# Weight sums written over the raw weights, two borrowed load buffers, and a written step order with 120 fast pairs

## The chip, the cores and the metric

The kernel runs on one core of a Trainium2 chip. The metric is the device time of one execution, in microseconds (us). PE is TensorE, which multiplies matrices; PEld is its weight load; DVE is VectorE, ACT is ScalarE, POOL is GpSimd; SP is SyncE, whose queue issues nearly all loads here.

## What is computed

One encoder layer over 256 tokens of width 4096, in float32. The input projection has 9792 columns; multi-head latent attention and dilated attention run beside each other; their gated outputs go through an output projection; a gated per-layer embedding follows.

```python
h = rms_norm(x, g_mix)
proj = h @ w_in                      # 4096 x 9792
c_q, c_kv, k_rope, gate_a, q_b, k_b, v_b, gate_b = split(proj)
y_a = rms_norm(mla_attention(...), g_out_mla) * silu(gate_a)
y_b = rms_norm(dilated_mixture_attention(q_b, k_b, v_b), g_out_dil) * silu(gate_b)
x = x + concat(y_a, y_b) @ w_out     # 4096 x 4096
gate = sigmoid(rms_norm(x, g_ple) @ w_ple_gate)   # 4096 x 4096
x = x + (p @ w_ple) * gate
return rms_norm(x, g_final)
```

## The kernel before

Every float32 matrix product is done with split numbers: a value is a high half `hi` (rounded by an ACT copy) and a low half `lo` (the rest, by a DVE subtraction), and `mm` (L263) makes one product of three matmuls, hi x hi, hi x lo and lo x hi. Weights arrive as raw float32 tiles of 128 rows x 1024 columns (512 KB) over SP's queue, into four tiles with the tag `raw` (`RAW = 4`, L1887). A step of the program is one such conversion and the matmuls that use it. `fetch`, `convert_one` and the loop at the end keep loads and conversions some steps ahead of the matmuls; converted halves lie in three tiles `wp` and in further tiles of the stage's ring.

The three large projections are cut into blocks of 1024 output columns (class `Block`): six for q, k and v of the dilated attention (two blocks for each), five for the latent and the gates, three of the output projection (the rest of it runs as `Chunk`s), four of the embedding's gate. A block has 32 rows of tiles, and its output is 2 halves of tokens (256 = 2 x 128) by 2 halves of columns (2 x 512), four products for each row of tiles. That is a plain step (`plain_step`). Two rows of tiles can instead be taken as a 2 x 2 block matrix product in Winograd's form, with seven products where plain steps take eight: a fast pair (`fast_steps`). It needs sums of the four parts of the raw weights, which DVE makes, and sums of the activations, which `add_sums` makes once for a stage and which need room. A pair is four steps: M1; M2 and M3; M5 and M7; M6 and M4. The products M1, M5, M6 and M7 go to banks of their own and are added into the four quarters when the block's last pair is done (`d_mid`, `gate_mid`, `out_mid`, `wide_mid`), the other banks at the block's end (`d_done`, `gate_done`, `out_done`, `wide_done`).

Before, the weight sums T[0] and T[1] went into tiles of their own: T5 and T6 in the q/k/v stage, B1 at the gates, B4 and Al1 in the output projection, Ah2 in the last one. The first step of a pair needs both raw tiles; it releases the first one once the step is converted, the second step releases the second:

```python
sub(T[0][:, 0], r[0][:, 1], r[0][:, 0])
sub(T[0][:, 1], r[0][:, 1], r[1][:, 1])
split(hi[:, 0], lo[:, 0], r[0][:, 0])
```

How many pairs a block has stands in lists (`FAST_QKV`, `FAST_G`, `FAST_O`, `FAST_P`), and `spread` orders pairs and plain steps by fixed costs. All instructions are written out by a planner: `Clock` holds a modelled time for each engine, and tasks (attention heads, block ends, sums) are woven between the steps when the modelled times let them.

In `d_mid` and `d_done` the sums of q, k, v and of the latent are scaled by the row's normaliser while they are added (scalar_tensor_tensor on DVE from the banks). In `gate_rest` the gain of the output norm is multiplied in with the gate, head by head.

## Time and profile before

| | before |
|---|---|
| median of 3 runs | 1899.48 us (1897.54 to 1899.76) |
| profiled execution, span | 1897.4 us |
| PE busy | 1878.5 us (99%), 9133 matmuls and transposes |
| PEld busy | 1579.8 us (83%) |
| DVE busy | 1696.8 us (89%), 2354 instructions |
| ACT busy | 1140.2 us (60%), 1543 instructions |
| DMA | 370.59 MB, mean 195 GB/s |

The span is from the first to the last instruction of the profiled execution. Matmuls are pipelined: the busy time of PE takes the modelled end of each, so that short waits between two of them do not show in it.

### The profile page before, as it was taken

Reading aid. Unit: us, or ns where it says so; the run is one execution under the profiler, and the core shown is the slowest. Engines: PE = TensorE matmul, PEld = TensorE weight load, DVE = VectorE, ACT = ScalarE, POOL = GpSimd, SP = SyncE. Lnnn points to the kernel's source line nnn. Section 1 sums busy time; section 2 is a strip of 40 time slices with the busy share of each in tenths; the row PEclk is TensorE's granted clock in tenths of the full one; section 3 lists DMA queues with packets and bytes.
Section 4 is the critical chain, followed back from the end, with each engine's and each line's share of the span. In section 5 each row is a group of like instructions: output and inputs, shape, how many; then the busy total and the mean of one; then the engine's idle time right before and its main releaser. Section 6 shows DMA issues by size and latency. Waiting matters only on the chain.

```text
span 1897.4 us, 25417 instructions
## 1 busy us (share of the span) xinstructions
PE 1878.5 (99%) x9133; PEld 1579.8 (83%) x9133; DVE 1696.8 (89%) x2354; ACT 1140.2 (60%) x1543; POOL 31.2 (2%) x41
## 2 busy tenths in 40 slices
PE   9999999999999999999999999999999999999997
PEld 7888888888899888888888999888888888888885
DVE  6999999899898989999998777999989989989897
ACT  7655656565588555556556556656655555666654
POOL 0000000000011000000000010100000000000000
PEclk9999999999999999999999999999999999999999
DMA  8666666666735566666667553576666666665665
GB/s 279 189 205 213 214 212 200 198 213 193 218 84 159 166 211 183 196 215 189 208 199 209 137 142 123 167 231 204 216 199 217 187 194 218 194 223 183 221 222 180
DMA packets 160871, 370.59 MB, mean 195 GB/s; under 512 B 29116, under 2 KB 70952, under 8 KB 160744
## 3 DMA queue, kind: packets, MB, share of 16 engines
q1 hardware_dynamic: 159896, 366.58, 62.0%
q0 software_dynamic: 512, 1.84, 0.3%
q8 instruction: 72, 1.18, 0.3%
q10 hardware_dynamic: 336, 0.54, 0.1%
q14 instruction: 55, 0.45, 0.1%
HBM read 364.72 MB, written 4.19 MB: 194 GB/s over the span
## 4 chain that ended last, share of the span: by engine, by line
PE 85%; DVE 10%; DMA 2%; issue 2%; ACT 1%; POOL 0%; DVEq 0%; ACTq 0%; POOLq 0%
PE m L177 49%; PE t L177 16%; PE s L177 11%; PE o L177 9%; DVE lo L177 3%; DVE B L177 3%; DVE T L177 2%; DVE Ah L177 1%; DMA raw<-in_w_ple_gate_dram 1%; DVE Al L177 1%; DMA raw<-in_w_in_dram 1%; ACT hi L177 0%; DVE st L177 0%; ACT B L177 0%; DVE B7b L177 0%
## 5 line engine op out<-in xcount | busy, mean ns | idle before, releaser
L177 ACT ACTIVATE hi<-raw 128x1024 fp32r<-128x1024 f32 (+2 forms) x396 | 378.9, 966 | 278.1 <-PE m L177 70.9
L177 DVE TENSOR_TENSOR lo<-raw,hi 128x1024 fp32r<-128x1024 f32 (+2 forms) x396 | 433.4, 1107 | 61.8 <-ACT hi L177 60.6
L177 PE MATMUL m<-hi,Ah 128*128 128x512 f32 (+2 forms) x659 | 247.2, 387 | 0.3 <-ACT hi L177 0.3
L177 DVE TENSOR_TENSOR B<-raw,B 128x1024 fp32r<-128x1024 f32 (+3 forms) x228 | 213.9, 947 | 20.5 <-ACT B L177 18.8
L177 PE MATMUL m<-hi,Al 128*128 128x512 f32 (+2 forms) x625 | 229.6, 380 | 0.0
L177 PE MATMUL m<-lo,Ah 128*128 128x512 f32 (+2 forms) x549 | 207.8, 379 | 1.4 <-DVE lo L177 1.3
L177 ACT ACTIVATE B<-raw 128x1024 fp32r<-128x1024 f32 (+2 forms) x142 | 135.3, 962 | 96.8 <-DMA raw<-in_w_in_dram 25.3
L177 PE MATMUL m<-hi,B 128*128 128x512 f32 (+1 forms) x524 | 179.0, 389 | 0.0
L177 PE MATMUL m<-B,Ah 128*128 128x512 f32 (+2 forms) x554 | 146.7, 359 | 0.6 <-DVE B7b L177 0.6
L177 PEld LDWEIGHTS m<-hi,Ah 128*128 128x128 f32 x659 | 124.0, 188 | 22.7 <-ACT hi L177 1.2
L177 PEld LDWEIGHTS m<-hi,Al 128*128 128x128 f32 x625 | 117.5, 188 | 21.8
L177 PEld LDWEIGHTS m<-lo,Ah 128*128 128x128 f32 x549 | 103.4, 188 | 19.9 <-DVE lo L177 2.9
L177 PEld LDWEIGHTS m<-hi,B 128*128 128x128 f32 x524 | 98.2, 188 | 19.6
L177 PEld LDWEIGHTS m<-B,Ah 128*128 128x128 f32 x554 | 95.9, 189 | 15.3 <-DVE B7b L177 1.0
L177 PE MATMUL m<-lo,B 128*128 128x512 f32 (+1 forms) x262 | 102.1, 390 | 0.1
L177 PE MATMUL m<-B,Al 128*128 128x512 f32 (+2 forms) x289 | 99.1, 371 | 0.0
L177 DVE TENSOR_TENSOR T<-raw,T 128x512 f32<-128x512 f32 (+2 forms) x110 | 85.5, 789 | 3.3 <-ACT T L177 1.7
L177 ACT ACTIVATE hi<-B 128x1024 fp32r<-128x1024 f32 x57 | 59.4, 1056 | 23.1 <-PE m L177 7.3
L177 DVE TENSOR_TENSOR lo<-B,hi 128x1024 fp32r<-128x1024 f32 x57 | 68.5, 1220 | 3.9 <-ACT hi L177 3.6
L177 PE MATMUL t<-hi,Ah 128*128 128x512 f32 x184 | 69.9, 391 | 0.0
L177 ACT ACTIVATE B<-T 128x1024 fp32r<-128x1024 f32 (+2 forms) x55 | 50.2, 916 | 22.8 <-DVE T L177 13.4
L177 PEld LDWEIGHTS m<-B,Al 128*128 128x128 f32 x289 | 54.4, 188 | 9.2
(530 smaller groups left out, 4336.9 us busy)
## 6 DMA issues: line engine op xcount, KB each, us to landing
raw<-in_w_in_dram SPq DMA_DIRECT2D x359, 512.0 KB, 4.3
raw<-in_w_out_dram SPq DMA_DIRECT2D x128, 512.0 KB, 4.6
raw<-in_w_ple_gate_dram SPq DMA_DIRECT2D x128, 512.0 KB, 4.7
raw_q<-in_w_uq_dram SPq DMA_DIRECT2D x32, 256.0 KB, 3.8
T<-in_x_dram SPq DMA_DIRECT2D x13, 512.0 KB, 6.6
raw<-in_w_in_dram SPq DMA_DIRECT2D x16, 320.0 KB, 3.1
raw_r<-in_w_uq_dram SPq DMA_DIRECT2D x16, 256.0 KB, 4.3
raw_k<-in_w_ukv_dram SPq DMA_DIRECT2D x16, 256.0 KB, 3.4
```

Source lines behind the costliest of these rows:

```text
L177: return do(out, *rest, **named)
```

## The change

The weight sums are written over the raw tiles: the first two (with plus signs, so the signs of the products M5 and M7 turn, which `mix` and `out_mid` take up) over the first raw tile, the other two over the second. A pair therefore keeps its first raw tile until its third step is converted, and its second until the fourth. Where the two raw tiles are neighbours, the first two sums are one instruction of 1024 columns. The first load of a pair belongs to its first step, the second to its second.

The four raw tiles are now parts of one tile; the tiles that held the sums are lent as two more raw buffers, from a point in each stage until the last pair of its last block has its loads (`lend`, `give_back`). `raw_slot` takes the buffer that the planner's clock has free first, or the neighbour of the pair's first one if that is free within 0.3 us.

`spread` goes; each block has its own written order, with c for a plain step and a, b, g, h for the four steps of a pair. The number of h gives 1, 8, 8, 8, 8, 8 pairs for q/k/v (before 3, 7, 8, 8, 8, 7), 3, 6, 8, 7, 8 for the latent and the gates (before 3, 6, 7, 7, 7), 6, 6, 7 for the output projection (before 6, 7, 6) and 8, 8, 8, 4 for the last one (before 7, 7, 7, 5): 120 in all, 116 before. A capital A would have made a sum by an adding load; no string has one. Sums of activations for which there is no tile go over the second token half of an activation whose pair needs it no more (`odd`). `add_sums` makes its four sums in three instructions and not four.

The scaling of q, k, v and the latent leaves the sums: `d_mid` and `d_done` add, and four scalings (on ACT, or on DVE when the planner's clock has DVE 0.3 us ahead) follow. The gain of the output norms moves into the activation that takes a head out of its bank, and `gate_rest` multiplies two heads at once. The last raw weights of the program are no longer converted into two raw tiles but into Ah3. The planner's clock now counts 0.4 us for an issue on SP and 2.3 us for a load to land.

```diff
+ORDER_D = (
+    "cccccccccccccccccaccbccccgcccchccc",
+    "ccccaabcbcgcgchhcaabbggcahhcbgachbghcaacbbgghhcc",
...
+ORDER_P = (
+    "cccaacbccbgghcchabgahccabgcbahcbgaghhbgacchbghcce",
...
+    raw_all = wp.tile([P, 2 * RAW, 512], F32, tag="raw", name="raw_all", bufs=1)
...
+    def raw_slot(after=None):
+
+        def when(at):
+            return clock.after(raw_tile(at), "sp", False, False)
+
+        best = min(raw_free, key=when)
+        if after is not None:
+            near = [at for at in raw_free if next_to(after, at)]
+            if near and when(near[0]) < when(best) + NEAR:
+                best = near[0]
+        raw_free.remove(best)
+        return best
...
+    def lend(stage, tags):
+
+        if lent["stage"] != stage:
+            give_back()
+            lent["stage"] = stage
+            for tag, n in tags:
+                t = slot(tag, [2 * n, 512])
+                for i in range(n):
+                    raw_at[lent["n"]] = t, 2 * i
+                    raw_free.append(lent["n"])
+                    lent["n"] += 1
...
+            def get1():
+                self.lend()
+                slots[0].append(raw_slot())
+                r.append(self.load(2 * j, slots[0][0]))
+
+            def get2():
+                slots[1].append(raw_slot(slots[0][0]))
+                r.append(self.load(2 * j + 1, slots[1][0]))
+                if self.closes == j:
+                    self.closed = True
+                    give_back()
...
             def split1(hi, lo):
-                if isinstance(self.tmp, tuple):
-                    T.extend(slot(b, [2, self.q]) for b in self.tmp)
+                split(hi[:, 0], lo[:, 0], r[0][:, 0])
...
-                sub(T[0][:, 0], r[0][:, 1], r[0][:, 0])
-                sub(T[0][:, 1], r[0][:, 1], r[1][:, 1])
-                split(hi[:, 0], lo[:, 0], r[0][:, 0])
...
-                nc.scalar.activation(hi, r[1], AF.Copy)
-                sub(T[1][:, 0], r[1][:, 1], T[0][:, 0])
-                sub(T[1][:, 1], r[1][:, 0], T[1][:, 0])
+                if next_to(slots[0][0], slots[1][0]):
+                    t, h = raw_at[slots[0][0]]
+                    plus(r[0], t[:, h + 1:h + 2].to_broadcast([P, 2, self.q]), t[:, h:h + 4:3])
                 else:
...
+                    plus(r[0][:, 0], r[0][:, 1], r[0][:, 0])
+                    plus(r[0][:, 1], r[0][:, 1], r[1][:, 1])
                 nc.vector.tensor_tensor(lo, r[1], plain(hi), op=ALU.subtract)
+                sums34()
+
+            def sums34():
+                plus(r[1][:, 1], r[1][:, 1], r[0][:, 0])
+                plus(r[1][:, 0], r[1][:, 0], r[1][:, 1])
...
+            new = [
+                self.step("M1", get1, split1, run((0, "M1", A11)), needs, 0, 0.69),
+                self.step("M2 M3", get2, split2, run((0, "M2", A12), (1, "M3", S(3))), needs, 0, 1.37),
+                self.step("M5 M7", None, split3, run((0, "M5", S(2)), (1, "M7", S(0))), more, 1, 1.37),
+                self.step("M6 M4", None, lambda hi, lo: split(hi, lo, r[1]), run((1, "M6", S(1)), (0, "M4", A22)), more, 1, 1.37),
             ]
...
-                nc.vector.scalar_tensor_tensor(d[h][:, t], blk.ps[m], sc[t], d[h][:, t], op0=ALU.mult, op1=ALU.add)
+                nc.vector.tensor_tensor(d[h][:, t], blk.ps[m], d[h][:, t], op=ALU.add)
+            yield from awaited("rx")
+            for m, t, h in quarters[2:] + quarters[:2] if key == ("v", 1) else quarters:
+                if clock.free["dve"] + 0.3 < clock.free["act"]:
+                    nc.vector.tensor_scalar(d[h][:, t], d[h][:, t], sc[t], None, op0=ALU.mult)
+                else:
+                    nc.scalar.activation(d[h][:, t], d[h][:, t], AF.Copy, scale=sc[t])
...
-    PLACES = "B5", "Ah2", "Al2", "B0", None, None, None, ""
+    PLACES = "B5", "Ah2", "Al2", "B0", None, None, None, "Ah3"
```

## Rows read from the trace of the kernel before

**Rows 1.** The page: span, busy time, share and instructions of each engine.
```profile
span 1897.4 us, 25417 instructions
...
PE 1878.5 (99%) x9133; PEld 1579.8 (83%) x9133; DVE 1696.8 (89%) x2354; ACT 1140.2 (60%) x1543; POOL 31.2 (2%) x41
```

**Rows 2.** Chain that ended last: start, length, what; one unbroken run of matmuls.
```profile
347.35 10.88 PE m L177 x48
```

**Rows 3.** Busy time by 20 us slices: PE, PEld, DVE, ACT, POOL, granted clock, DMA.
```profile
80.00:100.00 20.00, 19.72 (x87) 16.00 (x87) 19.52 (x38) 11.72 (x13) 0.00 (x0) 1.00 0.63 204
100.00:120.00 20.00, 19.96 (x88) 16.05 (x87) 19.79 (x32) 10.40 (x15) 0.00 (x0) 1.00 0.64 198
...
180.00:200.00 20.00, 19.39 (x86) 15.74 (x85) 19.93 (x25) 9.60 (x12) 0.00 (x0) 1.00 0.67 218
...
340.00:360.00 20.00, 20.00 (x90) 16.57 (x89) 18.25 (x23) 9.69 (x12) 0.00 (x0) 1.00 0.65 210
...
1240.00:1260.00 20.00, 19.72 (x88) 15.95 (x87) 19.73 (x29) 10.49 (x13) 0.00 (x0) 1.00 0.69 232
...
1580.00:1600.00 20.00, 19.97 (x88) 16.04 (x87) 19.86 (x23) 13.02 (x14) 0.00 (x0) 1.00 0.69 219
...
1840.00:1860.00 20.00, 19.69 (x87) 15.90 (x87) 17.08 (x19) 10.43 (x11) 0.00 (x0) 1.00 0.81 266
```

**Rows 4.** The same view for longer stretches: q/k/v, gates, last projection, tail.
```profile
40.00:180.00 140.00, 139.68 (x624) 114.69 (x623) 135.49 (x211) 84.22 (x113) 0.00 (x0) 1.00 0.64 198
...
720.00:1020.00 300.00, 300.00 (x1341) 248.45 (x1340) 278.55 (x333) 177.39 (x193) 0.00 (x0) 1.00 0.66 198
...
1540.00:1800.00 260.00, 259.97 (x1146) 214.52 (x1145) 237.43 (x283) 157.60 (x183) 0.00 (x0) 1.00 0.65 208
...
1884.00:1897.40 13.40, 0.11 (x1) 0.00 (x0) 7.94 (x24) 4.70 (x9) 0.00 (x0) 0.68 0.72 276
```

**Rows 5.** Timeline of DVE in a gate block: start, length, instruction, count, idle before.
```profile
886.97 0.69 DVE L177 TENSOR_TENSOR B<-raw 128x512 f32<-128x512 f32 x1
887.58 0.69 DVE L177 TENSOR_TENSOR B<-raw,raw 128x512 f32<-128x512 f32 x1
...
892.39 1.22 DVE L177 TENSOR_TENSOR B7b<-B,B7a 128x1024 fp32r<-128x1024 f32 x1
893.52 1.22 DVE L177 TENSOR_TENSOR lo<-B,hi 128x1024 fp32r<-128x1024 f32 x1
894.78 0.69 DVE L177 TENSOR_TENSOR B<-raw 128x512 f32<-128x512 f32 x1
```

**Rows 6.** DVE instructions by shape: count, busy us, mean ns, idle before.
```profile
L177 DVE TENSOR_TENSOR lo<-raw,hi 128x1024 fp32r<-128x1024 f32 x309 | 374.0, 1220 | 59.4 <-ACT hi L177 58.3
...
L177 DVE SCALAR_TENSOR_TENSOR B<-m,st,B 128x512 f32<-128x512 f32 x26 | 17.8, 742 | 0.1
...
L177 DVE TENSOR_TENSOR B<-B,m 128x512 f32<-128x512 f32 x20 | 12.7, 681 | 0.1
...
L177 DVE SCALAR_TENSOR_TENSOR Ah<-Ah,gT,t 128x256 f32<-128x256 f32 x8 | 3.5, 476 | 0.7 <-PE t L177 0.7
```

**Rows 7.** ACT instructions by shape, the same columns.
```profile
L177 ACT ACTIVATE hi<-raw 128x1024 fp32r<-128x1024 f32 x309 | 323.8, 1058 | 240.9 <-PE m L177 64.7 <-DMA raw<-in_w_in_dram 52.7 <-PE t L177 48.1
...
L177 ACT ACTIVATE T<-T,st 128x512 f32<-128x512 f32 x8 | 5.3, 709 | 0.8 <-DVE st L177 0.8
```

**Rows 8.** What SP's load queue waited for: us in total, times, longest.
```profile
SPq L177 <- DVE lo L177: 960.6, 400, 10.1
```

**Rows 9.** The chain that ended last, 145 to 186 us.
```profile
160.99 4.89 DMA raw<-in_w_in_dram
...
184.54 1.65 PE m L177 x6
```

**Rows 10.** DMA issues: count, KB each, median us to landing.
```profile
raw<-in_w_in_dram SPq DMA_DIRECT2D x359, 512.0 KB, 4.3
```

**Rows 11.** What ACT waited for, 40 to 500 us: us in total, times, longest.
```profile
ACT hi L177 <- DMA raw<-in_w_in_dram: 34.2, 19, 5.8
```

More of the change, by code (lines that the diff above doesn't have):

```diff
@@ L129, in run @@
             queue = "dma", engine
-            self.free[queue] = max(self.free.get(queue, 0.0), at + 2.0) + late
+            self.free[queue] = max(self.free.get(queue, 0.0), at + self.LANDS[engine]) + late
             seen = self.free[queue]
@@ L1185, in product, with lend, load @@
             tick()
-        def load(self, kt):
+        def lend(self):
+            if lent["stage"] != self.stage[0] and not self.closed and self.lend_ready():
+                lend(*self.stage[:2])
+        def load(self, kt, at):
             kt = self.row(kt)
-            r = clock.made(wp.tile([P, 2, self.q], F32, tag="raw", name=f"raw_{kt}", bufs=RAW), "raw", RAW)
+            r = raw_tile(at, (2, self.q))
             for lo, n in ((0, Q), (Q, Q)) if self.late and kt == 16 else ((0, 2 * self.q),):
@@ L1360, in z_dst @@
     def z_dst(j):
+        if j > 6:
+            return odd(*(x1T[c] for c in range(2 * j - 14, 2 * j - 12)))
         if j == 0:
@@ L1517, in both @@
                 END["kept"].append((hi, lo))
-            new = Step(lambda: box.append(blk.load(kt)), both, lambda hi, lo: part(0, j), [], 1, 0.69 * (1 + (j >= SKEW)))
+            new = Step(get, both, lambda hi, lo: part(0, j), [], 1, 0.69 * (1 + (j >= SKEW)))
+            new.slots = slots
             new.halves = lambda: place(j)
```

284 lines of the change are left out of this document (164 added, 120 removed).

## The prediction

> **What bounds the kernel now.** I read the page's busy table first, then the busy time in slices of 20 us, then the chain of waits for the slices that lose time, and only then the costs of single VectorE instructions.
>
> The busy table [rows 1] has PE at 1878.5 us of a span of 1897.4 us and DVE at 1696.8 us. What stands outside the span I carry along unchanged: the median of the runs is 1899.48 us, 2.1 us over the profiled span, so a span of S reads as S + 2.1 us.
>
> PE is the bound, and it is a bound of issue. A run of 48 matmuls of 512 columns takes 10.88 us in the chain [rows 2], which is 0.2267 us for one. A slice of 20 us in which nothing is missing has 16.57 us of weight load, as the one at 340 us [rows 3]; a slice with less has lost time even where PE reads 20.00, since the modelled end of a matmul covers a short wait. The loss of a slice is its shortfall against 16.57 us, times 20/16.57: 0.69 us at 80, 0.63 at 100, 1.00 at 180, 0.75 at 1240, 0.64 at 1580, 0.81 at 1840 [rows 3]. That makes 4.5 us, and the first three, 2.3 us, belong to the q/k/v stage. [...] At the end, from 1884.0 us to 1897.4 us, PE has one matmul left [rows 4]: 13.4 us of tail that the change leaves as it is.
>
> So the change can gain in two ways only: fewer matmuls, or fewer of these 4.5 us.
>
> **The change part by part.** *Pairs.* A plain pair of weight rows needs 8 products of 3 matmuls, a fast pair 7. The old lists hold 41 + 30 + 19 + 26 = 116 fast pairs, the new strings (one h for each) 41 + 32 + 19 + 28 = 120. Four products fewer are 12 matmuls, 12 x 0.2267 = **2.72 us** off PE. Nothing covers them, since PE issues without pause, so all of it leaves the path.
>
> *VectorE for the pairs.* One pair and one plain step lie between the starts at 886.97 and 894.78 us [rows 5]: 7.81 us. A 1024-wide operation starts 1.13 us before the next one (892.39 to 893.52), so the plain step is 1.13 us and the pair 6.68 us. A pair in place of two plain steps adds 6.68 - 2.26 = 4.42 us of DVE, four of them 17.7 us. In the new form the first two sums are one 1024-wide operation where the two load buffers are neighbours. Two 512-wide ones start 0.61 us apart, 1.22 us for both, against 1.13: 0.09 us saved a pair, between 0 (never neighbours) and 120 x 0.09 = 10.8 us. I take 8 us, since the code prefers a neighbour that is free within 0.3 us.
>
> [...]
>
> *Scaling of q, k, v and the latent.* The five scalar_tensor_tensor of the middle sums and four of the end (742 ns [rows 6]) become eight plain additions of two tensors (681 ns) and four scalings of 512 columns, which the planner gives to ACT unless its clock has DVE ahead. On DVE a block saves 9 x 0.742 - 8 x 0.681 = 1.23 us, seven blocks 8.6 us. On ACT they are four times 709 ns [rows 7]; ACT is at 60% [rows 1]. The gate product goes from 32 operations of 256 columns (476 ns) to 16 of 512 (681 ns): 4.3 us saved. The gain now rides on an activation that was there. Both are work beside PE. DVE in all: 17.7 - 8 - 8.6 - 4.3 = -3 us, that is, the same total with four more pairs. It costs PE nothing as long as converted weights are waiting.
>
> *Where it lands.* From 40 to 180 us DVE is busy 135.49 of 140 us, 96.8%; from 720 to 1020 278.55 of 300, 92.9%; from 1540 to 1800 237.43 of 260, 91.3% [rows 4]. The first q/k/v block goes from 3 pairs to 1, the second from 7 to 8: -4.4 us, and two block ends -2.5 us, leaves 128.6 of 140, 92%. The gates get two pairs: 278.6 + 8.8 - 2 (merges) over 300 - 1.4: 95.5%. The last projection's first three blocks get one each: 237.4 + 13.3 - 2 over 260 - 2: 96.3%. Load is moved from where PE waits to where it does not.
>
> *Six load buffers for four.* The load queue waits for VectorE: 960.6 us in 400 waits for the low halves alone [rows 8]. The chain behind the stall at 184 us has this loop in it: a buffer is loaded from 160.99 for 4.89 us, ACT waits for it, DVE waits for ACT and reaches the block's sums, whose banks PE wants, late; PE goes on at 184.54 [rows 9]. A landing takes 4.3 us in the median [rows 10]. With 32 loads in the 81.6 us of a block of eight pairs (16 steps of 2.72 us and 8 pairs of 4.76), one load is due every 2.55 us: four buffers may each be held 10.2 us, six 15.3 us. But a pair now keeps its first buffer until its third step and its second until its fourth. At 1.7 us a step and three to four steps between, that adds some 6 us to a pair's hold. With 4.3 us of landing and some 3 us of conversion (1.06 us on ACT [rows 7], 1.22 us on DVE [rows 6], and an estimate of what lies between): plain 7.3, pair 13.3, mean 10.3 us, where before it was 7.3 of 10.2. The slack goes from 2.9 to 5.0 us. So loads come earlier, and ACT's waits for raw weights (34.2 us for one group between 40 and 500 us [rows 11]) shrink. SP's queue also carries the residual and gain loads; they stand behind the weight loads as before and gain from a queue that waits less. The step that starts a pair now needs one landed load, not two. No read of PE hangs on the overwritten buffers; what overwrites them, on DVE, stands behind DVE's own low half, which waited for ACT's read.
>
> *Value taken for the 4.5 us.* Ends: all of it back (-4.5), or the dense blocks lose as the q/k/v stage did (+3.2 against the 2.3 back, below). I take the 2.3 us of q/k/v back, since DVE there falls to the 92% at which the gates lost nothing, and +0.6 us in the denser blocks, since the loads that fed the old stalls come earlier. **Sum: -2.72 - 2.3 + 0.6 = -4.4 us**, a span of 1893.0, a time of **1895.1 us**.
>
> **The rivals.** *The waits move.* DVE at 96% in the last projection loses what 96.8% lost in q/k/v: 1.32 us (slices 80 and 100) in 140 us, so 2.4 us in 258 us, 1.8 more than now, and the gates half that rate, 1.4 us. For: the same share of DVE. Against: the buffers. -2.72 - 2.3 + 3.2 = -1.8: 1897.7 us.
>
> *The buffers run short* (the slower one). The hold of a pair is set by the distance from first to third and second to fourth step in the strings; the place is each block of eight pairs, the point is a mean hold of 15.3 us. Beyond it a block lasts 32 x hold / 6: at 15.6 us it is 1.6 us longer, ten such blocks 16 us, so 1895.1 + 16 = 1911 us. Against: 10.3 us is far from 15.3. For: some strings start two pairs at once (aa), which holds four of six.
>
> *ACT is held at the block ends.* The new scalings on ACT wait for DVE's additions, and the conversions of the next weights queue behind them. If each of seven ends costs PE what the late sums cost at 184 us (1.0 us), it is 1895.1 + 7 = 1902 us. [...]
>
> *It does less than it says.* The lent buffers come too late to matter and no stall goes: only the matmuls, 1896.8 us.
>
> **How the numbers follow.** What a measurement of this kernel can tell from no change is about 0.2%, 3.8 us: faster lies under 1895.7, slower over 1903.3 us. The forecast has 0.52 (of it 0.44 under 1895.7, as its own spread is from 1892.2, all 4.5 us back, to 1896.5), the moved waits 0.27 (0.04 under), the short buffers 0.07, ACT held 0.07 (0.03 over), less than it says 0.07. Faster 0.48, same 0.42, slower 0.10. The range for 8 in 10 runs from 1891.0, under the best case by the spread of the runs, to 1901.0, which takes in the moved waits and most of the held ACT and leaves out the short buffers.
>
> **What would show it.** Right: 12 matmuls fewer on PE; 16.5 us of weight load in the slices at 80, 100 and 180; DVE near 1694 us; SP's waits and ACT's waits for raw weights clearly smaller; slices from 1540 to 1780 still at 16.5. Moved waits: shortfalls there and in the gates. Short buffers: ACT's waits for raw loads grow, with DVE idle beside them. ACT held: high halves waiting behind a scaling at the ends of q/k/v blocks. I am wrong if PE's time outside matmuls falls by more than 4.5 us or grows, or if the tail after the last matmul is no longer 13.4 us.

## The result and the profile after

| | before | after |
|---|---|---|
| median of 20 runs each | 1899.47 us | 1902.01 us |
| profiled execution, span | 1897.4 us | 1900.0 us |
| last matmul ends | 1884.1 us | 1887.4 us |

The ratio is 1.0015, with a 95% interval of 1.0009 to 1.0021: the change costs 2.5 us. The forecast was 1895.1 us and its range ended at 1901.0, so it was wrong in direction and the time lies outside the range, though the difference is smaller than the 0.2% that the prediction called the limit of one measurement.

The page of the kernel after, with the columns of [rows 1]:

```profile
span 1900.0 us, 25485 instructions
...
PE 1879.1 (99%) x9121; PEld 1577.5 (83%) x9121; DVE 1723.3 (91%) x2319; ACT 1162.9 (61%) x1576; POOL 30.8 (2%) x41
```

The twelve matmuls are gone (9133 to 9121), but DVE has 26.5 us more where 3 us less were forecast. The slices of 20 us of the kernel after, in the columns of [rows 3]:

```profile
80.00:100.00 20.00, 20.00 (x90) 16.57 (x89) 19.28 (x42) 10.48 (x16) 0.00 (x0) 1.00 0.65 201
100.00:120.00 20.00, 20.00 (x90) 16.57 (x89) 18.66 (x24) 12.37 (x15) 0.00 (x0) 1.00 0.38 111
180.00:200.00 20.00, 20.00 (x90) 16.57 (x89) 19.73 (x25) 12.75 (x16) 0.00 (x0) 1.00 0.48 170
...
800.00:820.00 20.00, 19.84 (x86) 15.71 (x85) 19.66 (x24) 12.39 (x13) 0.00 (x0) 1.00 0.62 206
840.00:860.00 20.00, 19.63 (x86) 15.91 (x86) 19.83 (x24) 10.80 (x12) 0.00 (x0) 1.00 0.76 250
...
1420.00:1440.00 20.00, 18.81 (x82) 14.62 (x80) 18.97 (x22) 12.31 (x14) 0.00 (x0) 1.00 0.68 228
1580.00:1600.00 20.00, 19.63 (x87) 15.94 (x86) 19.83 (x21) 12.50 (x13) 0.00 (x0) 1.00 0.60 190
```

The three slices of the q/k/v stage that had lost time are full at 16.57 us of weight load. The stalls now stand in the gates (800, 840), the output projection (1420) and the last projection (1580). The same view for the long stretches of [rows 4]:

```profile
40.00:180.00 140.00, 140.00 (x628) 115.81 (x627) 134.03 (x198) 86.39 (x116) 0.00 (x0) 1.00 0.63 206
720.00:1020.00 300.00, 299.13 (x1328) 245.49 (x1327) 287.49 (x335) 178.58 (x195) 0.00 (x0) 1.00 0.60 198
1540.00:1800.00 260.00, 259.05 (x1137) 212.59 (x1136) 250.60 (x295) 160.62 (x185) 0.00 (x0) 1.00 0.63 207
1887.40:1900.00 12.60, 0.01 (x1) 0.00 (x0) 7.84 (x24) 4.70 (x9) 0.00 (x0) 0.64 0.76 291
```

To compare stages I take PE's loss directly from the matmuls of each trace: from the start of one matmul to the next, less 0.2267 us for 512 columns or 0.1205 us for 256 (most of them start 0.226 to 0.227 and 0.120 us apart in the traces of before and after), summed where more than 0.025 us is left; matmuls of other widths, the transposes among them, are left out. Each row is one profiled execution, whose time can lie 1 to 2 us off the median of its kernel (`free` 1896.98 against 1895.53 us, `best4` 1898.25 against 1900.23 us), so differences of a few tenths say nothing.

| PE's loss, us | 40-510 | 510-640 | 640-1025 gates | 1025-1225 | 1225-1480 output | 1540-1800 last | all |
|---|---|---|---|---|---|---|---|
| before | 2.29 | 2.29 | 1.08 | 5.24 | 2.29 | 0.51 | 19.1 |
| after | 0.46 | 3.45 | 3.48 | 5.97 | 4.08 | 2.57 | 25.2 |
| after with two self-waits fewer in a pair (run `free`) | 0.46 | 3.43 | 1.40 | 6.22 | 2.71 | 1.02 | 20.6 |
| after without the fourth sum (`three`) | 0.46 | 3.20 | 1.07 | 6.08 | 1.92 | 0.00 | 17.1 |
| before with one self-wait more in a pair (`b_self`) | 2.66 | 2.30 | 1.28 | 5.18 | 4.07 | 1.92 | 22.5 |
| after, fourth sum behind the low half (`best3`) | 3.06 | 4.46 | 13.91 | 5.50 | 9.50 | 4.15 | 49.0 |

So the account of the span is: 12 matmuls less, -2.7 us; loss 6.1 us more; tail 12.6 us in place of 13.3, -0.7: together +2.7, and the span rose by 2.6 us. What has to be explained are the 6.1 us.

Where they come from is seen in the chain that ended last, in the third block of gates (start, length, what):

```profile
800.23 0.70 DVE raw_all L207
800.96 0.69 DVE raw_all L207
801.65 1.15 DVE B L207
802.82 0.70 DVE B L207
...
844.68 0.69 DVE B L207
845.37 1.15 DVE lo L207
846.56 0.73 PE o L207 x2
```

From 793.32 to 846.56 us the chain is almost DVE alone: no load is in it, and 1.6 us of ACT. PE waits at its end because VectorE has not come round. The instructions of DVE, in a gate block, with the columns of [rows 5]:

```profile
887.76 0.69 DVE L207 TENSOR_TENSOR raw_all<-raw_all 128x512 f32<-128x512 f32 x1
888.49 0.69 DVE L207 TENSOR_TENSOR raw_all<-raw_all,B 128x512 f32<-128x512 f32 x1
889.09 1.22 DVE L207 TENSOR_TENSOR lo<-B,hi 128x1024 fp32r<-128x1024 f32 x1
890.35 0.69 DVE L207 TENSOR_TENSOR B<-B,raw_all 128x512 f32<-128x512 f32 x1
891.07 0.69 DVE L207 TENSOR_TENSOR B<-B 128x512 f32<-128x512 f32 x1
891.68 1.22 DVE L207 TENSOR_TENSOR lo<-raw_all,hi 128x1024 fp32r<-128x1024 f32 x1
```

These are the four sums and the low half of a pair's second step. The second sum overwrites the half that the first one read, and starts 0.73 us after it; the operation after it, which has nothing to do with it, starts 0.60 us later. The third sum overwrites what the low half read: 1.26 us from start to start, against 1.14 for the unrelated ones at 891.68 (the next starts at 892.82). The fourth reads what the third wrote: 0.72 us. Before, the first two sums went to tiles of their own and started 0.61 us apart [rows 5]; only the fourth read the third's result. I call the 0.12 us a self-wait: VectorE waits for its own previous instruction. Written in place, a pair has three, before it had one. The trace also lists which semaphores (counters) an instruction waits for and which it counts up: the second, third and fourth sum wait for the one that VectorE itself counts up, the two low halves do not.

### The profile page after: what moved, and what is told of

Its sections match the earlier page's. It is cut to its first block, busy times and chain, and to the rows that moved or that the text cites. A ratio compares the mean times of both kernels' runs of the same rounds, so it can differ in the third digit from the quotient of the medians.

```text
span 1900.0 us, 25485 instructions
## 1 busy us (share of the span) xinstructions
PE 1879.1 (99%) x9121; PEld 1577.5 (83%) x9121; DVE 1723.3 (91%) x2319; ACT 1162.9 (61%) x1576; POOL 30.8 (2%) x41
## 4 chain that ended last, share of the span: by engine, by line
PE 73%; DVE 18%; issue 4%; DMA 3%; ACT 2%; DVEq 0%; ACTq 0%
PE m L207 43%; PE t L207 15%; PE s L207 9%; PE o L207 7%; DVE lo L207 7%; DVE raw_all L207 3%; DVE B L207 3%; DVE T L207 2%; DVE Al L207 1%; DVE Ah L207 1%; DMA raw_all<-in_w_ple_gate_dram 1%; DMA raw_all<-in_w_out_dram 1%; DVE B7b L207 1%; ACT hi L207 1%; DMA raw_all<-in_w_ple_dram 1%
## 5 line engine op out<-in xcount | busy, mean ns | idle before, releaser
L207 ACT ACTIVATE hi<-raw_all 128x1024 fp32r<-128x1024 f32 (+2 forms) x420 | 412.4, 995 | 233.4 <-PE m L207 49.1
L207 DVE TENSOR_TENSOR lo<-raw_all,hi 128x1024 fp32r<-128x1024 f32 (+2 forms) x420 | 473.9, 1146 | 58.8 <-ACT hi L207 57.3
L207 PE MATMUL m<-hi,Ah 128*128 128x512 f32 (+2 forms) x714 | 267.0, 388 | 0.0
L207 PE MATMUL m<-lo,Ah 128*128 128x512 f32 (+2 forms) x590 | 223.9, 379 | 1.1 <-DVE lo L207 1.0
L207 ACT ACTIVATE B<-raw_all 128x1024 fp32r<-128x1024 f32 (+2 forms) x146 | 142.6, 982 | 81.2 <-PE m L207 19.8
L207 DVE TENSOR_TENSOR raw_all<-raw_all 128x512 f32<-128x512 f32 (+1 forms) x252 | 183.3, 728 | 7.4 <-DMA raw_all<-in_w_in_dram 1.0
L207 DVE TENSOR_TENSOR B<-raw_all,B 128x1024 fp32r<-128x1024 f32 (+2 forms) x146 | 163.8, 1127 | 5.0 <-ACT B L207 4.5
L207 PEld LDWEIGHTS m<-hi,B 128*128 128x128 f32 x490 | 91.8, 188 | 18.6 <-DVE B L207 0.5
L207 ACT ACTIVATE hi<-B 128x1024 fp32r<-128x1024 f32 (+1 forms) x62 | 62.4, 1009 | 48.1 <-PE t L207 13.4
L207 DVE TENSOR_TENSOR lo<-B,hi 128x1024 fp32r<-128x1024 f32 (+1 forms) x62 | 71.4, 1159 | 3.8 <-ACT hi L207 3.8
L207 PE MATMUL t<-lo,Ah 128*128 128x512 f32 x173 | 67.3, 389 | 0.0
```

The lines of the kernel that those rows point to most:

```text
L207: return do(out, *rest, **named)
```

## The experiments

Two theories: **self-waits** (VectorE's longer sums make its bursts end later, and PE waits for them) and **lateness** (a sum stands in the wrong place in VectorE's queue, and ACT, which converts the summed tile next, or VectorE behind it, is held). A third, **density**: one pair more in a block is what VectorE cannot carry there.

**1. The sums moved apart, with the planner free to weave anew (`nowar`).**

```diff
-                    plus(r[0][:, 1], r[0][:, 1], r[1][:, 1])
                 nc.vector.tensor_tensor(lo, r[1], plain(hi), op=ALU.subtract)
-                sums34()
+                if not both:
+                    plus(r[0][:, 1], r[0][:, 1], r[1][:, 1])
...  (in the third step)
+                plus(r[1][:, 1], r[1][:, 1], r[0][:, 0])
                 nc.vector.tensor_tensor(lo, r[0], plain(hi), op=ALU.subtract)
+                plus(r[1][:, 0], r[1][:, 0], r[1][:, 1])
```

> Edit: the changed kernel with VectorE's work of a pair in another order, the same operations: first sum, low half of the second tile, second sum in the second step; third sum, low half of the first tile, fourth sum in the third step. No sum then overwrites or reads what the instruction just before it touched. Theory A (VectorE waits for its own previous instruction when it overwrites what that one reads, 0.73 us from start to start where independent ones take 0.61; some 20 us in all, and the dense blocks run short of VectorE): DVE busy falls from 1723 by 15 to 25 us, the loss of PE after 640 us falls by at least 3 us, time 1897 to 1899 us. Theory B (it is the four more pairs and their place, not how their sums are written): DVE falls too, but less than 1.5 us of time comes back. Theory C (the buffers are held too long, loads come late): no change of time, 1901 to 1903 us.

Measured: 1927.79 us, ratio to before 1.0150 (1.0136 to 1.0164). VectorE did fall, to 1701.2 us, 22 less than in the change, and the time rose by 26 us. Less work on VectorE was no gain in itself here; experiment 5 finds which of the moved sums did it.

**2. More merged sums, and the old strings (`near`, `sparse`, `sparse4`).** `near` takes the neighbouring buffer always; `sparse` gives the changed kernel the orders that `spread` made before, with 116 pairs; `sparse4` is that without the two lent buffers.

```diff
-    RAW, NEAR = 4, 0.3
+    RAW, NEAR = 4, 100.0
... (sparse: every string as spread made it, as here the last v block)
-    "ccaccabgbcghhcabghcabgchacbgabahgcchbcabcgghhccc",
+    "ccccacbcghacbghacbcghabcghabcghacbghacbghccccc",
... (sparse4, besides)
-            for tag, n in tags:
+            for tag, n in ():
```

> Edit: the changed kernel takes the neighbouring buffer for a pair's second load whenever it is free, however late (0.3 us made 100 us in the planner's choice). The trace of the changed kernel has some 19 to 23 merged sums of 1024 columns for 120 pairs. Theory A: each further merged pair saves 0.73 + 0.61 - 1.14 = 0.2 us of DVE, so with 60 or more further merges DVE falls by 12 us or more and 1 to 3 us of time come back. Theory C: a worse choice of buffer makes loads later and the time 1 us or more longer. Theory B: within 1 us of the changed kernel.

> Edit: the changed kernel with the 116 pairs of the kernel before, in the order that its spread function gives (a b g h for its four fast steps); sums over the raw weights, lent buffers and moved scalings stay. PE gets 12 matmuls more, 2.72 us. Theory B: the dense blocks are the cause; PE's loss after 640 us falls by 6 us or more and the time by 3 to 6 us, to 1896 to 1899 us. Theory A: VectorE still waits for itself in each pair; of the 25.2 us that PE loses in the changed kernel 2 to 4 us go, and with 2.72 us more of matmuls the time is 1901 to 1904 us. Theory C: loads stay late, time 1903 us or more.

> Edit: as the run with 116 pairs in the old order, and without the two lent buffers: four raw buffers, each pair holding two of them until its third and fourth step. Theory C (buffers bind) says at least 5 us more than with six buffers. Theories A and B say that VectorE sets the pace and loads wait for it anyway: within 2 us of the run with six buffers. What I take for the likelier: 3 to 8 us more, as a pair then holds half of the buffers.

Measured: `near` 1905.38 us (1.0028, 1.0019 to 1.0037), with 4.3 us less on VectorE; 40 of the 120 pairs are merged in it, where the change has 19. Its median is 3.4 us longer, and ACT's waits for weights on their way rose from 140 to 166 us: waiting for a neighbour costs more than the merge brings. `sparse` 1911.05 us (1.0060, 1.0048 to 1.0073). `sparse4` 2018.46 us (1.0622, 1.0607 to 1.0636). What ACT waited for, first in `sparse`, then in `sparse4` (us in total, times, longest):

```profile
ACT hi L207 <- DVE raw_all L207: 86.8, 62, 3.0
...
ACT B L207 <- DVE raw_all L207: 47.1, 27, 4.5
```

```profile
ACT hi L207 <- DMA raw_all<-in_w_in_dram: 125.6, 81, 3.9
...
ACT hi L207 <- DMA raw_all<-in_w_ple_gate_dram: 62.3, 35, 3.3
```

With four buffers the in-place sums starve ACT of loads: all its waits for weights on their way come to 402 us, against 182 before and 140 in the change. With six, in the old order, loads are no trouble (39 us in all), but ACT waits 156 us for the sums in the four own buffers, since the second, third and fourth step of a pair follow each other closely ("bghc", "bcgh"); in the change it is 57 us. So the two lent buffers are worth 107 us to this scheme, and the written strings, which pull a pair's steps apart and have four pairs more, another 9 us. The strings do not cause the loss; without them it would be larger.

**3. One pair less in the dense blocks (`fewer`), and single sums moved (`mild`, `early`).**

```diff
-    "cccccabcccgahbgabachghbgccabhcgabhghcabcagbghhcc",
+    "cccccabcccgahbgabcchghcccabcgabhghcabcagbghhcc",
... (so too the fifth gate string and the first three of the last projection)
... (mild: one line moved)
-                    plus(r[0][:, 1], r[0][:, 1], r[1][:, 1])
                 nc.vector.tensor_tensor(lo, r[1], plain(hi), op=ALU.subtract)
+                if not next_to(slots[0][0], slots[1][0]):
+                    plus(r[0][:, 1], r[0][:, 1], r[1][:, 1])
... (early: the first sum behind the first step's split, none merged)
                 split(hi[:, 0], lo[:, 0], r[0][:, 0])
+                plus(r[0][:, 0], r[0][:, 1], r[0][:, 0])
```

> The changed kernel with seven pairs where it has eight in the third and fifth block of the gates and the first three of the last projection, the fourth pair of each string turned into two plain steps; five products more for PE, 5 x 0.68 = 3.4 us. Density theory: the loss of the gates goes from 3.5 to the 1.1 us of the kernel before and that of the last projection from 2.6 to 0.5, so 1902.0 + 3.4 - 4.5 = 1901 us, the extra pairs having gained nothing. Self-wait or latency theory: the stalls sit in the other pairs too, the losses go down by a sixth at most, 1904.5 to 1905.5 us.

> The changed kernel with one sum moved behind the low half of the pair's second step: sum 1 of the first raw tile, low half of the second, sum 2 of the first, sums of the second; all four sums stay in that step. It breaks one of the three places where a VectorE operation overwrites what the one just before it read, in the some 100 pairs without a merged sum. Self-wait theory: 100 x 0.11 = 11 us less VectorE (1723 to about 1712) and the loss of the gates, the output projection and the last projection (3.5 + 4.1 + 2.6 us) falls by a third: 1898.5 to 1900 us. Rival, latency of the sums: the low half now waits for ACT uncovered and the sums come 0.5 us later, so ACT's waits for the sums (37 + 15 us) grow past 65 us and the time rises to 1904 us or more. Rival, density of pairs: no change, 1901 to 1903 us.

> The changed kernel with the first of the four sums in the pair's first step and no merged sums. Latency theory (the second step hands VectorE 3.8 us in one burst, and the third step's conversion and what queues behind it on ACT wait for that): ACT's waits for the sums fall from 52 us to under 35 us, and the time to 1898 to 1900 us although VectorE has some 2 us more work. Self-wait theory: the number of self-waits is the same and the merged sums are gone, 1902 to 1904 us.

Measured: `fewer` 1902.85 us (1.0024, 1.0014 to 1.0034), `mild` 1904.29 us (1.0034, 1.0021 to 1.0048), `early` 1905.68 us (1.0039, 1.0026 to 1.0051). `fewer` is 115 pairs in place of 120; VectorE fell from 1723.3 to 1699.5 us, 4.8 us a pair. The loss in the gates fell from 3.48 to 1.78 us and in the last projection from 2.57 to 1.71, 2.6 of the 4.5 us that density alone would give back, and the whole loss by 2.6 us against 3.4 us of added products. By the medians the five pairs are still worth 0.8 us, a quarter of their 3.4 us, but the intervals of `fewer` and of the change overlap, so that they gain anything is not shown (the planner also wove the tasks anew in `fewer`). `early` speaks against lateness of the first sum by one figure, ACT's waits for the sums, which stayed at 57 us. Its time cannot be read, and that of `mild` neither: in both the output projection was woven anew, and a single stall there (2.89 us in `early`, 2.66 us in `mild`), with slower matmuls behind it, outweighs the rest; in `early` these are 4.7 us, more than the 3.7 us by which its loss rose. From here on the planner's clock is shown the sums of the changed kernel (`like`, `skip` and `quiet` in the wrapper of the engines: the clock counts other operands than are given, an instruction that isn't given, or nothing), so that a kernel keeps its own order.

**4. The self-waits alone, at the same order (`free`, `three`, `b_self`).**

```diff
-                    plus(r[0][:, 0], r[0][:, 1], r[0][:, 0])
+                    plus(r[0][:, 0], r[0][:, 0], r[0][:, 0], [r[0][:, 1], r[0][:, 0]])
-                nc.vector.tensor_tensor(lo, r[1], plain(hi), op=ALU.subtract)
+                nc.vector.tensor_tensor(lo, r[0], plain(hi), op=ALU.subtract, like=[r[1], plain(hi)])
-                plus(r[1][:, 0], r[1][:, 0], r[1][:, 1])
+                plus(r[1][:, 0], r[1][:, 0], r[0][:, 0], [r[1][:, 0], r[1][:, 1]])
... (three: the changed kernel with)
-                plus(r[1][:, 0], r[1][:, 0], r[1][:, 1])
+                plus(r[1][:, 0], r[1][:, 0], r[1][:, 1], skip=True)
... (b_self: the kernel before with)
-                sub(T[0][:, 1], r[0][:, 1], r[1][:, 1])
+                sub(T[0][:, 1], T[0][:, 0], r[1][:, 1], [r[0][:, 1], r[1][:, 1]])
```

> The changed kernel, every engine's instructions in the same order and of the same sizes; three operations of a pair's second step read other data, so that none reads or overwrites what the one just before it wrote or read (the first sum adds the first half to itself, the low half is taken from the first raw tile, the fourth sum reads the first tile's sum): the sums and so the output are not those of the reference. Self-wait theory: VectorE falls by about (2 x 100 + 2 x 120 - 80) x 0.11, some 30 us, from 1723 to 1690 to 1700, and the losses of the gates, the output and the last projection (3.5 + 4.1 + 2.6 us) go back to those before (1.1 + 2.3 + 0.5): 1902 - 6.3 = 1895.7 us. Rival, latency or late loads: VectorE falls as much, but the stalls stay, 1900.5 to 1902.5 us.

> The changed kernel without the fourth sum of each pair (its tile is used without it, so the output is not the reference's), all other instructions in the same order: 120 x 0.73 = 88 us less VectorE. If VectorE's load is what the stalls in the dense blocks hang on, nearly all of them go: at least 8 us of the 10.2 us in the gates, output and last projection, 1893 to 1895 us. If they hang on loads and buffers or on ACT's own queue: at least half stay, 1897 us or more.

> The kernel before, in its own order on all engines; the second sum of each pair reads the first sum's result in place of the raw half that this was made from (other values, so the output is not the reference's). One self-wait more in each of 116 pairs: VectorE 116 x 0.12 = 14 us more, 1697 to 1711. Self-wait theory, at the rate of 6.3 us of loss for 26.5 us of VectorE: +3 us, 1902.5 us. Rival, VectorE's load does not matter at this scale: 1899 to 1900 us.

`free` and `b_self` make other sums than the layer needs, and `three` leaves the fourth one out.

Measured: `free` 1895.53 us (0.9983, 0.9974 to 0.9991), `three` 1893.29 us (0.9967, 0.9954 to 0.9979), `b_self` 1902.66 us (1.0019, 1.0010 to 1.0028). The page of `free`:

```profile
PE 1876.3 (99%) x9121; PEld 1577.6 (83%) x9121; DVE 1704.7 (90%) x2319; ACT 1164.5 (61%) x1576; POOL 30.9 (2%) x41
```

As many instructions on every engine as in the change, and 18.6 us less on VectorE (30 were expected). The sums themselves did take 30.3 us less. But `free` isn't free of self-waits: its low half reads the half that the second sum has just written, which the expectation overlooked, and starts 0.79 us after that sum where it was 0.60 us. These low halves cost 11.2 us more:

```profile
887.33 0.69 DVE L207 TENSOR_TENSOR raw_all<-raw_all,B 128x512 f32<-128x512 f32 x1
888.12 1.23 DVE L207 TENSOR_TENSOR lo<-raw_all,hi 128x1024 fp32r<-128x1024 f32 x1
```

So `free` has one self-wait in a pair, as the kernel before had, and the change three. Slices of `free` in the stages that had lost time:

```profile
800.00:820.00 20.00, 20.00 (x89) 16.21 (x88) 19.61 (x24) 12.57 (x14) 0.00 (x0) 1.00 0.63 207
840.00:860.00 20.00, 20.00 (x90) 16.40 (x89) 19.83 (x24) 11.67 (x13) 0.00 (x0) 1.00 0.76 260
...
1580.00:1600.00 20.00, 20.00 (x90) 16.57 (x89) 19.69 (x23) 12.41 (x13) 0.00 (x0) 1.00 0.69 221
```

VectorE is as busy in them as in the change (19.83 us at 840 in both), but it gets further: the weight load is back at 16.2 to 16.57 us. The loss falls by 4.6 us of the 6.1, and by the medians `free` is 6.5 us faster than the change. The mirror image is `b_self`, whose pair begins so:

```profile
888.02 0.69 DVE L177 TENSOR_TENSOR B<-raw 128x512 f32<-128x512 f32 x1
888.74 0.69 DVE L177 TENSOR_TENSOR B<-B,raw 128x512 f32<-128x512 f32 x1
889.35 1.82 DVE L177 TENSOR_TENSOR lo<-raw,hi 128x512 fp32r<-128x512 f32 x2
```

0.72 us between two sums that started 0.61 us apart in [rows 5], once in each of 116 pairs: VectorE 1705.7 us, 8.9 more, and the loss 3.4 us more, 1.8 of it in the output and 1.4 in the last projection. That VectorE's own time is the main matter is shown from both sides. The gates need both: there one more self-wait in a pair alone adds 0.2 us (`b_self`), the added pairs without the added self-waits 0.3 us (`free`), and the change has 2.4 us more. `three`, with 73 us less on VectorE, brings the loss to 17.1 us, below that of the kernel before.

**5. Which late sum costs 26 us, and can the self-waits be had out (`nowarf`, `best3`, `best2`, `best4`, `mildf`)?** All in the order of the changed kernel, with the right sums at other places of VectorE's queue.

```diff
... (mildf, best2, best3, nowarf: the second sum behind the second step's low half)
... (best2, best4: the fourth sum in the third step, ahead of its low half)
+                plus(r[1][:, 0], r[1][:, 0], r[1][:, 1], quiet=True)
                 nc.vector.tensor_tensor(lo, r[0], plain(hi), op=ALU.subtract)
... (best3, nowarf: behind it; nowarf also has the third sum ahead of it)
                 nc.vector.tensor_tensor(lo, r[0], plain(hi), op=ALU.subtract)
+                plus(r[1][:, 0], r[1][:, 0], r[1][:, 1], quiet=True)
```

> The changed kernel with the second sum of a pair behind the low half, as in an earlier run, but with all other instructions in the order of the changed kernel (the planner's clock is not told of the swap). About 100 x 0.11 = 11 us less VectorE. Self-wait theory: a third of the 6.3 us that the dense blocks lost comes back, 1899.5 to 1900.5 us. Rival, the sums that come 0.5 us later hold ACT and so the next conversions: 1902 to 1904 us.

> The changed kernel with the second sum behind the low half of the second step and the fourth sum in the third step ahead of that step's low half; everything else in the order of the changed kernel, the output that of the reference. Two of three self-waits gone in the some 100 pairs without a merged sum, one of two in the others: about 200 to 220 x 0.11 = 22 to 24 us less VectorE (1723 to about 1700). Self-wait theory, at 6.5 us for the 30 us of the run without self-waits: -4.7 us, 1897.3 us. Rival, lateness: the third step's low half comes 0.6 us later and the second sum 1.1 us, which eats it: 1900 us or more.

> The same with the fourth sum behind the third step's low half, so that this low half is not held; the fourth step's conversion on ACT then waits for it where it follows at once. Self-wait theory: as many self-waits gone, 1897.3 us. Lateness: ACT's waits for the sums grow from 52 us towards the 135 us of the run with the third and fourth sums late, and the time to 1900 us or more.

> The first experiment's order of the sums (second behind the low half, third ahead of and fourth behind the third step's low half), but with all else in the order of the changed kernel. If the 26 us that the first experiment lost came from its other weaving of tasks between the steps: 1896 to 1898 us, as nearly no self-wait is left (VectorE about 1700). If they came from the sums being late for ACT's next conversions: ACT's waits for the sums stay near 135 us and the time at 1910 us or more.

> The changed kernel with the fourth sum alone moved, to the third step ahead of its low half; the second sum stays where it was, everything else in the order of the changed kernel. One self-wait less in 120 pairs, some 13 us less VectorE (1710). If moving the second sum (the run with that alone gained 0.7 us) only costs ACT: as fast as or faster than the run with both moved, 1898.5 to 1899.5 us. If both moves add up by their self-waits: 1900 to 1900.5 us.

| | moved | time, us | ratio to before | VectorE busy, us | VectorE's waits for high halves, us |
|---|---|---|---|---|---|
| after | none | 1902.01 | 1.0015 (1.0009 to 1.0021) | 1723.3 | 66.4 |
| `mildf` | second | 1901.27 | 1.0011 (1.0002 to 1.0020) | 1715.0 | 72.9 |
| `best4` | fourth, ahead of the low half | 1900.23 | 1.0004 (0.9995 to 1.0013) | 1718.2 | 66.4 |
| `best2` | second, and fourth ahead | 1899.25 | 1.0002 (0.9993 to 1.0011) | 1710.3 | 72.9 |
| `best3` | second, and fourth behind | 1927.00 | 1.0149 (1.0135 to 1.0163) | 1708.1 | 99.3 |
| `nowarf` | second, third, and fourth behind | 1925.84 | 1.0143 (1.0129 to 1.0157) | 1702.5 | 100.1 |

`nowarf` is as slow as `nowar`, so the weaving was not it. Between `best2` and `best3` one instruction has changed places with its neighbour, and that is 27.75 us. VectorE at one such pair in the gates, first in `best2`, then in `best3` (the last bracket is the idle time before an instruction, and what ended it):

```profile
750.74 0.69 DVE L207 TENSOR_TENSOR B<-B,raw_all 128x512 f32<-128x512 f32 x1
751.47 0.69 DVE L207 TENSOR_TENSOR B<-B 128x512 f32<-128x512 f32 x1
752.08 2.35 DVE L207 TENSOR_TENSOR lo<-raw_all,hi 128x1024 fp32r<-128x1024 f32 x2
```

```profile
748.80 1.41 DVE L207 TENSOR_TENSOR raw_all<-raw_all 128x512 f32<-128x512 f32 x2
750.69 1.23 DVE L207 TENSOR_TENSOR lo<-raw_all,hi 128x1024 fp32r<-128x1024 f32 x1 [0.48 <-ACT hi L207]
751.83 0.68 DVE L207 TENSOR_TENSOR raw_all<-raw_all 128x512 f32<-128x512 f32 x1
```

```profile
749.60 1.06 ACT L207 ACTIVATE hi<-raw_all 128x1024 fp32r<-128x1024 f32 x1 [2.95 <-DVE raw_all L207]
```

The last fence is ACT in `best3`. ACT may convert the first tile's sums when the second sum is done, and takes 1.06 us for it; VectorE's low half has to wait for that. In `best2` the third and fourth sums fill this time and VectorE never stops. In `best3` only the third is left to fill it, VectorE idles 0.48 us, and the fourth sum still has to come. Over the run VectorE's waits for high halves are 99.3 us in place of 72.9, 26.4 more, nearly the 27.75 us of the time. ACT's waits for the sums in the four own buffers grow as well, from 117 to 161 us, since the next step's conversion needs the fourth sum; which of the two waits sets the time is not separated, and both come from the place of this one sum. So lateness is real too, but it was not in the change as it stood: there all four sums stand in front of that low half. It also explains `nowar`: 22 us of busy time saved on VectorE, and 40.7 us of waiting added (107.1 us). `best2` and `best4` have medians 2.8 and 1.8 us below that of the change and end level with the kernel before; their intervals overlap that of the change, and that `best2` beats the kernel before is not shown.

**6. The scalings (`b_scale`, `best2s`).** `b_scale` is the kernel before with only the new sums and scalings of q, k, v and the latent; `best2s` is `best2` with two of the four scalings of the last v block on VectorE.

```diff
-                nc.vector.scalar_tensor_tensor(d[h][:, t], blk.ps[m], sc[t], d[h][:, t], op0=ALU.mult, op1=ALU.add)
+                nc.vector.tensor_tensor(d[h][:, t], blk.ps[m], d[h][:, t], op=ALU.add)
+            yield from awaited("rx")
+            for m, t, h in quarters[2:] + quarters[:2] if key == ("v", 1) else quarters:
+                if clock.free["dve"] + 0.3 < clock.free["act"]:
+                    nc.vector.tensor_scalar(d[h][:, t], d[h][:, t], sc[t], None, op0=ALU.mult)
+                else:
+                    nc.scalar.activation(d[h][:, t], d[h][:, t], AF.Copy, scale=sc[t])
... (best2s)
+                    u = key == ("v", 1) and h == 1
-                    nc.scalar.activation(d[h][:, t], d[h][:, t], AF.Copy, scale=sc[t])
+                    nc.scalar.activation(d[h][:, t], d[h][:, t], AF.Copy, scale=sc[t], skip=u)
+                    u and nc.vector.tensor_scalar(d[h][:, t], d[h][:, t], sc[t], None, op0=ALU.mult, quiet=True)
```

> The kernel before with the scaling of q, k, v and the latent alone taken over from the change: plain sums from the banks, four scalings behind them on ACT or VectorE. If this edit is what gave the q/k/v stage its time back: the loss from 40 to 510 us falls from 2.3 to under 1 us, VectorE by 5 to 9 us, 1897.5 to 1898.5 us. If the strings and the lent buffers did it: the loss stays at 2.3 us and the time at 1899 to 1900 us. If the scalings hold ACT at block ends: 1902 us or more.

> The run with the second and fourth sums moved (1899.25 us), and two of the four scalings at the end of the last v block on VectorE in place of ACT, the order otherwise kept. There the first head's copy on ACT queues behind four scalings and PE loses 1.2 us from 514 to 517 us. If ACT held by the scalings is that loss: it falls by about 1 us and the time to 1898.3 us. If the head is late for another reason: the stall stays and the time at 1899 to 1899.7 us.

Measured: `b_scale` 1899.18 us (1.0003, 0.9994 to 1.0012). VectorE fell by 5.1 us and ACT rose by 15.3, and the loss from 40 to 510 us stayed at 2.15 us. So it was not the scalings that gave the q/k/v stage its time back. The two lent buffers alone did not either: `sparse`, which has them with the old orders, lost 2.7 us there. It took the written orders, with their other number of pairs in the first blocks. What the scalings do cost shows at the end of the last v block of the change, on ACT and on PE:

```profile
511.68 2.56 ACT L207 ACTIVATE B<-B,st 128x512 f32<-128x512 f32 x4 [0.47 <-DVE B L207]
514.15 0.57 ACT L207 ACTIVATE T<-t 128x512 fp32r<-128x512 f32 x1
```

```profile
514.78 0.39 PE L207 MATMUL s<-T 128*128 128x256 f32 x1 [0.28 <-ACT T L207]
515.51 0.86 PE L207 MATMUL s<-T 128*128 128x256 f32 x5 [0.34 <-DVE T L207]
```

The first head's copy of T stands behind the four scalings in ACT's queue, and PE, which wants T next, loses 0.44 + 0.60 us there. Before, PE ran through this place without a wait. `best2s` came out at 1899.95 us (1.0007, 0.9998 to 1.0016), not the 1898.3 hoped for. PE in it at the same place:

```profile
516.53 0.86 PE L207 MATMUL s<-T 128*128 128x256 f32 x5 [1.49 <-DVE T L207]
```

The two scalings now hold the low half of T on VectorE, and the stall is longer. From 517.6 us on, 16 matmuls of 256 columns then start 0.21 us apart in place of 0.12; the granted clock of the 8 us from 516 us is 0.79. That is 1.5 us more, so the run also says little about what the shorter queue on ACT was worth. The place is tight on both engines; that the scalings are in it is shown, that moving them frees it is not.

## Why the prediction was wrong

- **Twelve matmuls less, 2.72 us:** right.
- **The q/k/v stage gets 2.3 us back:** right, 1.8 us from 40 to 510 us by the table, with the three slices at 16.57. Of the reasons given, `b_scale` takes the scalings away and `sparse` the buffers alone; what the pairs and what the order did is not told apart. VectorE did not fall to 92% there: 134.03 of 140 us are 95.7%, and no loss goes with it.
- **Six buffers, with 10.3 of 15.3 us held:** right in its result. Weights on their way hold ACT for 140 us in all where it was 182, and the buffers are not short; `sparse4` shows that they would be with four. That SP's waits would be clearly smaller was wrong, they are nearly what they were in [rows 8]:

```profile
SPq L207 <- DVE lo L207: 949.7, 404, 9.8
```

- **VectorE, -3 us in all:** the step that failed first. It measured +26.5. Term by term: four pairs at the 4.8 us a pair of `fewer` are 19.0 (forecast 17.7). The scalings are -5.1 by `b_scale` (forecast -8.6). The merges were taken as -8, for some 90 of 120 pairs; the trace has few:

```profile
L207 DVE TENSOR_TENSOR raw_all<-raw_all 128x512 f32<-128x512 f32 x234 | 161.3, 690 | 7.2 <-DMA raw_all<-in_w_in_dram 1.0
...
L207 DVE TENSOR_TENSOR raw_all<-raw_all 128x1024 f32<-128x1024 f32 x18 | 22.0, 1220 | 0.2
```

  These 18 and one more in a lent tile, 19 merged sums at 0.09 us, are -1.7. That the code prefers a neighbour that is free was no evidence that one is free: with six buffers and two pairs under way it seldom is. And a term of some +18.6 was missing, the two self-waits that the change adds to a pair (the difference to `free`, which has two fewer). The gate products, 32 before and 16 after, add up to 12.8 and 10.3 us of DVE's busy time in the two traces, -2.5 (forecast -4.3). This makes 19.0 - 5.1 - 1.7 + 18.6 - 2.5 = 28.3, somewhat more than the 26.5 measured; 0.6 us of it are the self-waits of the four added pairs, which are in two of the terms, and the rest is open. The prediction costed the new sums by the starts of the old ones, 0.61 us apart, and read them as the price of a sum. They were the price of two sums that do not touch each other's data; the sentence that no PE read hangs on the overwritten buffers asked who else waits, and not whether VectorE itself does.
- **+0.6 us in the denser blocks:** the step on which the time hangs. It measured +2.4 in the gates, +2.1 in the last projection and, where the number of pairs did not change, +1.8 in the output projection. The shares of VectorE that were forecast for the gates and the last projection came out nearly exactly (95.5% and 96.3%; 287.49 of 300 us are 95.8%, 250.60 of 260 us are 96.4%). That is luck in part, as the forecast had no self-waits in it. The price of such a share was wrong. It was taken as almost nothing because the stalls of before had a load in their chain and the loads come earlier now. `free` shows that with the same loads in the same order, and VectorE as busy as ever in the slices at 800 and 840, most of the stalls go; `fewer` shows that fewer pairs take back half of them. A share over 300 us does not show where VectorE falls behind: from 792.7 to 862.4 us it works without a pause of 0.15 us, and PE waits for it at the end of the chain shown above. Such a run alone is no sign of loss, though: from 411.3 to 497.1 us the change has a longer one at which PE loses nothing. The forecast also had no added loss in the output projection, and its list of losing slices, with its 4.5 us, passed over one there that was 1.1 us short by the prediction's own measure:

```profile
1420.00:1440.00 20.00, 19.71 (x86) 15.67 (x85) 17.48 (x20) 11.43 (x12) 0.00 (x0) 1.00 0.69 219
```

- **The rivals.** The waits moved, as the second case said: its 1.8 us for the last projection was 2.1, its 1.4 for the gates 2.4. It left out the output projection and the attention stages (+1.8 and +1.9), so its 1897.7 us was low too. The short buffers did not come. ACT held at block ends is there once, with 1.0 us from 514 to 516 us, not at seven ends.
- **The tail**, taken as unchanged at 13.4 us, is 12.6 us.

What stays open: of the 6.1 us, the added self-waits carry 4.6 (`free`; not apart from the pairs, as `fewer` takes back 2.6 by itself), and 1.0 us stands at the end of the last v block, behind the scalings. The 0.7 us that the attention stage from 1025 to 1225 us lost stay in `free` and `three` too; their cause has not been tried.

## What to carry to other kernels

Before an operation is written over its own input to save a tile, read in the trace how far apart dependent and independent neighbours start on that engine, and count the in-place ones; then either leave an unrelated instruction between them or take the cost into the sum. Count how often a conditional saving can apply (neighbouring free buffers) before giving it a term. And where two engines handed work to and fro here, the place of a short instruction mattered more than its length: the same 120 sums of 0.7 us, in front of the instruction that waits for the other engine or behind it, were 28 us apart, and leaving them out gained 8.7 us (`three`).

## What the runs showed of the hardware

**On VectorE an operation that touches its predecessor's data starts 0.12 us later.** Sums of 512 columns that last 0.69 us start 0.60 to 0.61 us apart when they share nothing that either writes, and 0.71 to 0.73 us apart when the second reads or overwrites what the first wrote or read; after an operation of 1024 columns that lasts 1.22 us it is 1.14 against 1.25 to 1.26 us. In the trace of the change the line between the two kinds is the wait for VectorE's own semaphore: of the 369 instructions that follow a 512-column float32 sum without it (and without a longer idle time), 359 start 0.60 to 0.61 us after it, and of the 296 with it, 281 start 0.71 to 0.73 us after it. No run leaves this wait out between two operations that share data, so whether VectorE would overlap them without it is not shown. By the rows of the change the first kind starts some 0.08 us before the one ahead has ended, and the second some 0.03 us after it.

**PE's clock fell after a pause of 2.7 us.** In `mild`, a stretch in the output projection (columns of [rows 3]) and PE's timeline in it:

```profile
1418.00:1426.00 8.00, 5.34 (x17) 4.00 (x16) 4.84 (x7) 3.47 (x5) 0.00 (x0) 0.79 0.53 186
```

```profile
1421.48 0.47 PE L207 MATMUL t<-hi,B 128*128 128x512 f32 x1 [2.66 <-DVE B L207]
...
1423.03 0.63 PE L207 MATMUL m<-hi,Ah 128*128 128x512 f32 x1
1423.46 0.63 PE L207 MATMUL s<-hi,B 128*128 128x512 f32 x1
```

After PE had waited 2.66 us, the granted clock of these 8 us is 0.79, and from 1422.6 to 1425.6 us seven matmuls start 0.43 us apart in place of 0.2267; the third and the fourth after the wait had still started 0.23 us behind the one ahead. It cost 1.4 us on top of the wait (7 x 0.2). `early` shows the same behind a pause of 2.89 us (0.81 from 1329 to 1337 us) and `best2s` behind one of 1.49 us (0.79 in the 8 us from 516 us). After the change's longest single stall, 1.1 us at 1428 us, the clock of the slice stays at 1.00, and in `mildf` it stays there for the 8 us that follow a pause of 1.54 us, so the length of the pause alone does not decide. In `mild` the stall cost more than its length, 2.66 us and 1.4 us behind it.
